# A two-layer hybrid backbone on one core: the first norm's rests all on VectorE and its values in place, the filter's products behind the modulation's, the first S5 steps' scratch below the filter

## The chip, the core and the metric

The kernel runs on one core of one Trainium2 chip. The time is device time of one execution in microseconds (us). Three runs of the kernel before took 1841.52 us (median; 1838.38 to 1842.83). A further execution was profiled: 1841.73 us, of which the trace spans 1839.8 us, so that 1.93 us lie around the span.

## The reference, cut to what matters

Two layers work on 256 context tokens and 256 latent tokens of width 1024, in float32. A vector of modulation values (shift, scale and gate for each half of a layer) comes from a small product with `ada_w`. The projected columns go to three mixers: a Fourier mix, a hyena mix (long convolutions whose filter is computed from weights) and S5 (a linear scan with complex states).

```python
for l in range(DEPTH):                                  # 2
    mod = silu(c) @ ada_w[l] + ada_b[l]                 # 6 rows of 1024, one set for each token kind
    h = modulate(rmsnorm(x, norm_mix_g[l]), sh_m, sc_m) # h * (1 + scale) + shift
    p = h @ w_in[l]                                     # to Fourier | hyena (3 x 384) | S5 (384)
    y = concat(fourier_mix(p_f), hyena_mix(p_h, k), s5(p_s)) @ w_out[l]
    x = x + g_m * y
    h = modulate(rmsnorm(x, norm_ffn_g[l]), sh_f, sc_f)
    x = x + g_f * (swiglu(h) if l == 0 else moe_top2_of_8(h))
return rmsnorm(x, final_g)

# hyena's filter: k = sine network of the position, times a decay, over its own sum of magnitudes
# S5: B_bar = ((exp(lam dt) - 1) / lam) * B, complex; h[t] = A_bar h[t-1] + B_bar u[t]; both directions
```

## The kernel before

**Numbers in two parts.** Layer 0's products are taken in three passes over rounded parts: a value x is held as xH (rounded) and xL = x - xH, its **rest**. The same holds for a weight (`wh`, `wl`; `wsplit`, L191 and L192). A product is hH.wh + hL.wh + hH.wl, so one column tile of the input projection is 24 matmuls of 512 columns (8 slices of the width, 3 passes). In the trace they are `pacc<-hH,wh`, `pacc<-hL,wh` and `pacc<-hH,wl`.

**The stages, by the trace.** 0 to about 62 us: the modulation's first rows (`ada_pe`, chunks 0, 2, 1, 3), the first half of hyena's filter (`hy_filter`), the first norm (`norm_h`) and S5's parameters (`s5_params`), whose tables of rotations `rotA` and `rotB` are one long chain of small operations on GpSimd. From 62 to about 295: layer 0's mixers (`mixers`): the projection's tiles m = 11, 12, 13 (S5's columns), 10, 2 and so on, S5 in sixths (`s5_mats` builds a sixth's matrices, `s5_sixth` runs its scan), and the hyena convolutions. To about 380: the out projection and the second norm; to about 800: the feed-forward part; to about 990: layer 1's mixers; to the end: eight experts, streamed from memory.

**What sets the order.** A scheduler of the tile framework puts each engine's instructions into one list, from the program's order and a cost model, and a list is worked strictly in its order. A tile taken from a pool that lies over a closed pool waits until all of the closed pool's readers and writers are done.

**The first norm** (`norm_h`, L468 to L503) holds its eight slices in `xin`. L492 multiplies them by 1/rms (VectorE). Then, for each slice: L499 (ScalarE) and L500 (VectorE) write the modulated values of the two token kinds into a tile `nf`, of which there are two; L501 (ScalarE) rounds it into `hH`; L502 subtracts into `hL`, on GpSimd and VectorE by turns.

**The filter** (`hy_filter`, L708 to L780) has two halves (one for each order). In each: two tiles of `hfb` (L753, VectorE), their sum `hs` and difference `hd` (L762, L763, GpSimd), the sum of magnitudes by TensorE (`psk<-ones,ab`), its reciprocal `rc` (L765, VectorE), the reciprocal spread by TensorE (`prk`) and copied to `rk` (L770, ScalarE), four products `pk` with `hs` and `hd` (TensorE), `Kf = pk * rk` (L777, VectorE), for two of the four an addition (L779, GpSimd), and a DMA to memory (L780, on SyncE's queue, `kd<-Kf`). Its pool `filt` is closed at the first S5 work, and the mixers' tiles `x2`, `U` and the ring `ar` of the modulation's later chunks lie over it.

**S5's sixth** (`s5_mats`): `bs`, `cs`, `d` are loaded (L566 to L568); L585 to L587 form `bre` and `bim` of 512 columns with a second product `x2` on GpSimd in layer 0 (L586; the trace calls the tile `x`); the scratch of these lies in a pool `scr` over S5's parameters' pool.
Of the kernel before, what the change touches and what calls it, by code (L numbers as in the profile page):

```python
# [8 lines left out]
F32 = mybir.dt.float32  # L9
# [7 lines left out]
D = 1024  # L17
# [118 lines left out]
def build(tc, A, out, dbg=None, upto='all'):  # L136
# [254 lines left out]
    def ada_pe(c, pool, cnt=[0]):  # L391
        pa = pt_('acc', (128, 512), "pad")
        for kh in range(2):
            cnt[0] += 1
            if cnt[0] % 2 or pool is None:
                r = load(A['adaN'][c][:, 4 * kh:4 * kh + 4], 4, 512)
            else:
                r = pool.tile([128, 4, 512], F32, name="raw2", tag="raw2", bufs=2)
                SP.dma_start(r, A['adaN'][c][:, 4 * kh:4 * kh + 4])
            for k in range(4):  # L400
                mm(pa[32 * k:32 * k + 32], scol32[:, 8 * kh + 2 * k:8 * kh + 2 * k + 32], r[:, k], kh == 0, kh == 1)
        row = (pool or wraw).tile([128, 512], F32, name="adr", tag="adr" if pool else "raw", bufs=1 if pool else 2)
        act(row, pa, AF.Copy)
        pt = pa[:, 0:8].rearrange("p (j s) -> p j s", s=2)
        for j in range(4):
            mm(pt[:, j], row[:, 128 * j:128 * j + 128], sum4, j == 0, j == 3, skip_group_check=True)
        act(mods[0][:, 4 * c:4 * c + 4], pt, AF.Copy)
        mods_done(0, 4 * c, 4)

# [19 lines left out]
    def ada(l, m0, m1, eng, pool):  # L429
        for m in range(m0, m1):  # L430
            r = pool.tile([128, D], F32, name="ar", tag="ar", bufs=2)
            SP.dma_start(r, A['adaT'][l, m])
            for s in range(1 if l == 1 and m >= 16 else 0, 2):
                o = mods[l][:, m, s:s + 1]
                if eng(m, s) == 'v':
                    jk = par.tile([128, D], mybir.dt.bfloat16, name="jk", tag="jk", bufs=1)
                    stt(jk, r, 1.0, crow[:, s], op0=mul, op1=mul, accum_out=o)
                else:
                    pd = par.tile([128, D], F32, name="pd", tag="pd", bufs=1)
# [28 lines left out]
    def norm_h(l, w, x, hH, hL, pool, inplace=False, **kw):  # L468
# [27 lines left out]
        for k in range(KD):  # L496
            u = us[k] if inplace else unit(k)
            f = tmp.tile([128, 512], F32, name="nf", tag="t512b", bufs=2)
            act(f[:, 0:256], u[:, 0:256], AF.Identity, bias=mods[l][:, sh0 + k, 0:1], scale=Gm[l][w][:, k, 0:1])  # L499
            ts_(f[:, 256:512], u[:, 256:512], Gm[l][w][:, k, 1:2], mods[l][:, sh0 + k, 1:2], op0=mul, op1=add)  # L500
            act(hH[:, k], f, AF.Copy)  # L501
            (gtt, tt_)[k % 2](hL[:, k], f, hH[:, k].bitcast(F32), op=sub)  # L502
# [55 lines left out]
    def s5_mats(p, l, q, M, rh, rd):  # L558
# [25 lines left out]
        for i, (src, op) in enumerate(((bre, sub), (bim, add))):  # L584
            tt_(src, bt(PB[0]), bh(bb[:, i]), op=mul)  # L585
            (tt_ if l else gtt)(x2, bt(PB[1]), bh(bb[:, 1 - i]), op=mul)  # L586
            tt_(src, src, x2, op=op)  # L587
            pt = pt_('mat', (128, 4, 128), "pbt")
            for g in range(4):
                PE.transpose(pt[:, g], src[:, g].rearrange("p t h -> p (t h)"), ident)  # L590
            act(M[:, :, 128 * i:128 * i + 128], pt, AF.Copy)
# [116 lines left out]
    def hy_filter(p, l, kd):  # L708
# [33 lines left out]
        for o_ in range(2):  # L742
# [40 lines left out]
    def mixers(l, hH, hL, z2, yH, yL, fill):  # L783
# [84 lines left out]
        def conv(p, K, src0, src1):  # L868
# [115 lines left out]
        with tc.tile_pool(name=f"s5p{l}", bufs=1, side="right") as p, banks(mat=2, s5=2):  # L984
# [36 lines left out]
            ysT = z2.tile([128, 3, n], F32, name="ysT", tag="ysT")  # L1021
# [16 lines left out]
            ms = [mats(0), mats(1)]  # L1038
# [5 lines left out]
            for th in range(3):  # L1044
                Y = p.tile([128, 4 if l == 0 else 2, 128], F32, name="Y")
                for h in range(2):
# [3 lines left out]
                    if l == 0 and q == 4:  # L1050
                        SC.close()
# [42 lines left out]
    z_es = ExitStack()  # L1094
    with tc.tile_pool(name="filt", bufs=1) as p_:
# [7 lines left out]
        with tc.tile_pool(name="prm", bufs=1) as p2_, tc.tile_pool(name="start", bufs=1) as st, banks(f=3, fk=1):  # L1103
# [9 lines left out]
            filt = hy_filter(p_, 0, kdr[0])  # L1113
# [13 lines left out]
    with z_es:  # L1127
# [3 lines left out]
        with tc.tile_pool(name="z0p", bufs=1) as z2, tc.tile_pool(name="ada0", bufs=1) as p_:  # L1131
# [9 lines left out]
            mixers(0, hH, hL, z2, yH, yL, fill0)  # L1141
# [689 lines left out]
```

## Time and profile before

| | |
|---|---|
| median of three runs | 1841.52 us |
| profiled execution | 1841.73 us, span 1839.8 us |
| TensorE busy (PE; PEld is its weight load) | 1714.5 us, 93% |
| VectorE (DVE) | 805.9 us, 44% |
| ScalarE (ACT) | 429.4 us, 23% |
| GpSimd (POOL) | 518.4 us, 28% |
| granted TensorE clock, mean over the span | 0.965 |

SyncE (SP) issues DMAs. The shares are means over stages with different limits. The granted clock is 1.0 at 2.4 GHz and 0.5 at 1.2 GHz. A row of a timeline holds the start, the duration, the engine, the line, the operation, out<-in, and in square brackets how long the engine was idle before it and for whom it waited. Nearly all matmuls have line L148, that of a helper, so they are told apart by their tiles.

### The profile page before, as it was taken

The page shows a single profiled execution, that of the slowest core. Times are in us where ns is not written, and L with a number is a line of the kernel's source. Part 1 is how long each engine was busy: PE and PEld are TensorE (multiplying, and loading weights), DVE is VectorE, ACT ScalarE, POOL GpSimd, SP SyncE. Part 2 cuts the span into 40 slices and gives each one's busy share as a digit, 9 for nine tenths or more (in the row PEclk, how much of TensorE's full clock was granted, in tenths as well). Part 3 has the DMA queues.
Part 4 walks back from the last instruction along what each step waited for, and adds up shares of the span by engine and source line. Part 5 has one row for each costly group of instructions (what it writes and reads, how often), then busy time and mean ns, then how long its engine had stood idle before and what let it go on. Part 6 is the DMA issues. An engine that isn't in the chain of part 4 may idle for free. (4 is left out here: it accounts for less than half of the span.)

```text
span 1839.8 us, 47195 instructions
## 1 busy us (share of the span) xinstructions
PE 1714.5 (93%) x20825; PEld 1193.8 (65%) x20825; DVE 805.9 (44%) x1502; ACT 429.4 (23%) x776; POOL 518.4 (28%) x512
## 2 busy tenths in 40 slices
PE   7988899899998998999998999999999989999984
PEld 4665667867766776788777656666666656666642
DVE  7589968875776667363853001111111101011102
ACT  4332324455444443232231000000000000000001
POOL 5965535567877676000420000000000000000000
PEclk7998999999999999999998999999999999999998
DMA  8244345434557555354649999999999999999994
GB/s 297 87 116 126 94 148 177 144 106 145 168 180 248 190 194 194 120 162 141 191 150 419 405 394 418 419 420 419 419 419 418 419 419 419 418 413 413 412 419 160
DMA packets 145461, 506.80 MB, mean 275 GB/s; under 512 B 18590, under 2 KB 71648, under 8 KB 101216
## 3 DMA queue, kind: packets, MB, share of 16 engines
q1 hardware_dynamic: 145248, 503.70, 72.0%
q8 instruction: 165, 2.70, 0.6%
q14 instruction: 48, 0.39, 0.1%
HBM read 489.34 MB, written 14.32 MB: 274 GB/s over the span
## 5 line engine op out<-in xcount | busy, mean ns | idle before, releaser
L148 PE MATMUL pgu<-raw,xe 128*32 128x256 f32 x9408 | 528.2, 379 | 12.2 <-DMA raw<-in_mwp_dram 11.4
L148 PEld LDWEIGHTS pgu<-raw,xe 128*32 128x32 f32 x9408 | 316.3, 110 | 209.5 <-DMA raw<-in_mwp_dram 15.1
L1652 DVE TENSOR_TENSOR sg<-sg,pgu 128x384 f32<-128x384 f32 (+1 forms) x56 | 28.2, 504 | 629.8 <-ACT sg L1651 629.8
L148 PE MATMUL py<-raw,hT 128*32 128x256 f32 x4704 | 270.0, 379 | 8.3 <-DMA raw<-in_mwp_dram 8.2
L440 POOL TENSOR_TENSOR pd<-ar,crow 128x1024 f32<-128x1024 f32 x88 | 226.6, 2575 | 105.4 <-ACT pd L441 83.9
L1547 POOL TENSOR_TENSOR ob<-ob,fgb 128x512 f32<-128x512 f32 x1 | 1.3, 1262 | 880.4 <-ACT ob L1546 880.4
L148 PEld LDWEIGHTS py<-raw,hT 128*32 128x32 f32 x4704 | 156.0, 110 | 110.4 <-DMA raw<-in_mwp_dram 7.9
L192 DVE TENSOR_TENSOR wl<-raw,wh 128x1024 fp32r<-128x1024 f32 x95 | 169.2, 1783 | 72.4 <-ACT wh L191 70.5
L1651 ACT ACTIVATE sg<-pgu 128x384 f32<-128x384 f32 (+1 forms) x56 | 25.2, 450 | 705.6 <-PE pgu L148 705.6
L148 PE MATMUL pgu<-fhL,wh 128*128 128x512 f32 (+1 forms) x376 | 146.2, 389 | 5.1 <-DVE fhL L538 5.1
L148 PE MATMUL pgu<-fhH,wh 128*128 128x512 f32 (+1 forms) x392 | 147.6, 387 | 1.4 <-ACT sg L1283 0.8
L148 PE MATMUL pgu<-fhH,wl 128*128 128x512 f32 (+1 forms) x360 | 142.1, 396 | 3.3 <-DVE wl L192 3.3
L191 ACT ACTIVATE wh<-raw 128x1024 fp32r<-128x1024 f32 x95 | 99.9, 1054 | 147.1 <-PE pacc L148 67.3
L441 ACT ACTIVATE pd<-pd 128x1024 f32<-128x1024 f32 x88 | 93.0, 1057 | 123.9 <-POOL pd L440 121.1
L148 PE MATMUL pacc<-HH,wh 128*128 128x512 f32 (+1 forms) x192 | 76.8, 401 | 14.2 <-DVE xT L1227 10.0
L148 PEld LDWEIGHTS pgu<-fhL,wh 128*128 128x128 f32 x376 | 72.2, 192 | 22.9 <-DVE fhL L538 6.4
L148 PEld LDWEIGHTS pgu<-fhH,wh 128*128 128x128 f32 x392 | 74.0, 193 | 16.6 <-issue 1.1
L148 PEld LDWEIGHTS pgu<-fhH,wl 128*128 128x128 f32 x360 | 68.1, 189 | 23.0 <-issue 4.7
L148 PE MATMUL pacc<-HL,wh 128*128 128x512 f32 (+1 forms) x192 | 74.6, 389 | 0.0
L148 PE MATMUL pacc<-HH,wl 128*128 128x512 f32 (+1 forms) x192 | 73.7, 390 | 0.3 <-DVE wl L192 0.3
L148 PE MATMUL pacc<-h,wm 128*128 128x256 f32 x272 | 64.5, 391 | 1.2 <-ACT h L549 1.2
L148 PEld LDWEIGHTS pacc<-h,wm 128*128 128x128 f32 x272 | 51.5, 194 | 9.0 <-ACT h L549 1.4
(583 smaller groups left out, 2410.8 us busy)
## 6 DMA issues: line engine op xcount, KB each, us to landing
raw<-in_mwp_dram SPq DMA_DIRECT2D x336, 1024.0 KB
ar<-in_adaT_dram SPq DMA_DIRECT2D x64, 512.0 KB
raw<-in_fwg_dram SPq DMA_DIRECT2D x11, 1024.0 KB
raw<-in_fwu_dram SPq DMA_DIRECT2D x11, 1024.0 KB
raw<-in_fwd_dram SPq DMA_DIRECT2D x11, 1024.0 KB
raw<-in_adaN_dram SPq DMA_DIRECT2D x8, 1024.0 KB
ar<-in_adaN_dram SPq DMA_DIRECT2D x16, 512.0 KB
raw<-in_w_out_dram SPq DMA_DIRECT2D x8, 1024.0 KB
```

Of the source, the lines that this page charges most:

```text
L148: return PE.matmul(o, l, r, start=start, stop=stop, **kw)
L191: act(h, r, AF.Copy)
L192: tt_(l, r, h.bitcast(F32), op=sub)
L440: gtt(pd, r, crow[:, s], op=mul)
L441: act(pd, pd, AF.Copy, accum_out=o)
L1547: gtt(o_, o_, fgb[:, hs], op=mul)
L1651: act(sg[:, 0:n], p[:, 0:n, 0:128], AF.Silu)
L1652: tt_(sg[:, 0:n], sg[:, 0:n], p[:, 0:n, 128:256], op=mul)
```

## The change

The parts below are made at once.

- `norm_h`: the modulated values are written into `xin` itself (no `nf`), and all eight rests are on VectorE. Its last rest is handed out as `done`.
- `s5_mats`: the two products `x2` of the first sixth are on VectorE.
- `hy_filter`: layer 0's products `pk` of both halves may be issued only behind the last matmul of `ada_pe(3)` (`sum4`; the trace writes `pad<-sum,adr`). Its sine network's scratch shares places with `ab`, `hd`, `hs`.
- A new pool `u0` below the filter's pool holds `U`, `ysT`, the scratch of `s5_mats` and the first hyena tiles' temporaries (four tiles with one buffer each that share places with `bre`, `x2`, `bim`, `y2`). The pool `scr` is gone. The matrices of the first two sixths are issued behind `done`.
- `ada`'s scratch (`jk`, `pd`) moves into the pool that its caller hands in.

```diff
@@ ada_pe
-            mm(pt[:, j], row[:, 128 * j:128 * j + 128], sum4, j == 0, j == 3, skip_group_check=True)
+            last = mm(pt[:, j], row[:, 128 * j:128 * j + 128], sum4, j == 0, j == 3, skip_group_check=True)
...
+        return last
@@ ada
-                    jk = par.tile([128, D], mybir.dt.bfloat16, name="jk", tag="jk", bufs=1)
+                    jk = pool.tile([128, D], mybir.dt.bfloat16, name="jk", tag="jk", bufs=1)
...
@@ norm_h
-            f = tmp.tile([128, 512], F32, name="nf", tag="t512b", bufs=2)
-            act(f[:, 0:256], u[:, 0:256], AF.Identity, bias=mods[l][:, sh0 + k, 0:1], scale=Gm[l][w][:, k, 0:1])
-            ts_(f[:, 256:512], u[:, 256:512], Gm[l][w][:, k, 1:2], mods[l][:, sh0 + k, 1:2], op0=mul, op1=add)
-            act(hH[:, k], f, AF.Copy)
-            (gtt, tt_)[k % 2](hL[:, k], f, hH[:, k].bitcast(F32), op=sub)
+            act(u[:, 0:256], u[:, 0:256], AF.Identity, bias=mods[l][:, sh0 + k, 0:1], scale=Gm[l][w][:, k, 0:1])
+            ts_(u[:, 256:512], u[:, 256:512], Gm[l][w][:, k, 1:2], mods[l][:, sh0 + k, 1:2], op0=mul, op1=add)
+            act(hH[:, k], u, AF.Copy)
+            rest = tt_(hL[:, k], u, hH[:, k].bitcast(F32), op=sub)
+        done.append(rest)
@@ s5_mats
-            (tt_ if l else gtt)(x2, bt(PB[1]), bh(bb[:, 1 - i]), op=mul)
+            (tt_ if l or q == 0 else gtt)(x2, bt(PB[1]), bh(bb[:, 1 - i]), op=mul)
@@ hy_filter
-            a = p.tile([64, 256], F32, name=nm + "a", tag="sina")
+            a = p.tile([64, 256], F32, name=nm + "a", tag="ab")
...
-                for t in range(2):
-                    mm(pk, fck[:, t, f // 2, (f % 2) * 128:(f % 2) * 128 + 128],
-                       (hs if f < 2 else hd)[:, t], t == 0, t == 1)
+                with tc.issue_after(after[0].ins) if after else nullcontext():
+                    for t in range(2):
+                        mm(pk, fck[:, t, f // 2, (f % 2) * 128:(f % 2) * 128 + 128],
+                           (hs if f < 2 else hd)[:, t], t == 0, t == 1)
@@ mixers
-            SC = ExitStack()
-            if l == 0:
-                scr = SC.enter_context(tc.tile_pool(name="scr", bufs=1, side="right"))
-            U = z2.tile([128, S5G, 4, 16], F32, name="U", tag="ysT")
+            U = (scr or z2).tile([128, S5G, 4, 16], F32, name="U", tag="ysT")
...
-            ms = [mats(0), mats(1)]
+            with tc.issue_after(behind.ins) if behind else nullcontext():
+                ms = [mats(0), mats(1)]
@@ the start
+    u0 = u_es.enter_context(tc.tile_pool(name="u0", bufs=1))
     with tc.tile_pool(name="filt", bufs=1) as p_:
...
+            after.append(ada_pe(3, st))
...
-            mixers(0, hH, hL, z2, yH, yL, fill0)
+            mixers(0, hH, hL, z2, yH, yL, fill0, u0, done[0])
+        u_es.close()
```

The engines' lists differ up to the middle of layer 0's feed-forward part and are the same behind it. Three places follow.

TensorE, around the first rest; `pad<-sum_88,adr` is `sum4` of `ada_pe(3)`. Before, then now:

```order
L148 MATMUL pk<-hs,ck 128x384 x3
L148 MATMUL pk<-hd,ck 128x384 x2
L148 MATMUL pad<-sum_88,adr 128x2 x4
L148 MATMUL pacc<-hH,wh 128x512
L148 MATMUL prk<-ident,rc 128x128 x3
L148 MATMUL pacc<-hL,wh 128x512
```
```order
L148 MATMUL pad<-sum_88,adr 128x2 x4
L148 MATMUL pk<-hs,ck 128x384 x4
L148 MATMUL pk<-hd,ck 128x384 x2
L148 MATMUL pacc<-hH,wh 128x512 x2
L148 MATMUL prk<-ident,rc 128x128 x3
L148 MATMUL pacc<-hL,wh 128x512
```

The modulation's last sum now stands ahead of all of the filter's products, one of which stood earlier before.

GpSimd, end of the rotation chain (`rtu`, `rtv`, `rotA`) and the filter's second half (the memset of `hfb`, then `hs` and `hd` twice). Before, then now:

```order
L755 MEMSET hfb 1x384
...
L762 TENSOR_TENSOR hs<-hfb 128x384
L763 TENSOR_TENSOR hd<-hfb 128x384
...
L762 TENSOR_TENSOR hs<-hfb 128x384
L248 TENSOR_TENSOR rotA<-rtu,rtv 128x48x2
L763 TENSOR_TENSOR hd<-hfb 128x384
...
L247 TENSOR_TENSOR rtv<-rotA,gen 128x192
L623 TENSOR_TENSOR M<-rotA,rotB 128x4x64 x4
L248 TENSOR_TENSOR rotA<-rtu,rtv 128x48x4
```
```order
L247 TENSOR_TENSOR rtv<-rotA,gen 128x192
L756 MEMSET hfb 1x384
L624 TENSOR_TENSOR M<-rotA,rotB 128x4x64 x2
L248 TENSOR_TENSOR rotA<-rtu,rtv 128x48x4
L763 TENSOR_TENSOR hs<-hfb 128x384
L764 TENSOR_TENSOR hd<-hfb 128x384
L596 TENSOR_TENSOR M<-cs,PC_108 128x4x128
L599 TENSOR_TENSOR M<-bb,PC_109 128x4x128
...
L763 TENSOR_TENSOR hs<-hfb 128x384
L764 TENSOR_TENSOR hd<-hfb 128x384
```

The filter's second half stood inside the chain and now stands behind all of it, and its second pair behind part of the first sixth's matrices.

VectorE, from the filter's second reciprocal to its first `Kf` (before), and from the last rests to the same place (now). `u`, `bb`, `bre`, `bim`, `x` and `M` belong to the first sixth:

```order
L765 RECIPROCAL rc<-psk 128x3
...
L585 TENSOR_TENSOR bre<-PB_106,bb 128x512
L248 TENSOR_TENSOR bb<-u_1115,u_1116 128x64
L585 TENSOR_TENSOR bim<-PB_106,bb 128x512
L192 TENSOR_TENSOR wl<-raw,wh 128x1024
L597 TENSOR_TENSOR M<-M,y_1125 128x4x128
...
L777 TENSOR_TENSOR Kf<-pk,rk 128x384 x2
```
```order
L502 TENSOR_TENSOR hL<-xin,hH 128x512 x2
L243 TENSOR_TENSOR u_1107<-bs,wre 128x64
...
L586 TENSOR_TENSOR bre<-PB_106,bb 128x512
L248 TENSOR_TENSOR bb<-u_1107,u_1108 128x64
L587 TENSOR_TENSOR x_1116<-PB_107,bb 128x512
L586 TENSOR_TENSOR bim<-PB_106,bb 128x512
...
L766 RECIPROCAL rc<-psk 128x3
L601 TENSOR_TENSOR M<-M,y_1117 128x4x128
L192 TENSOR_TENSOR wl<-raw,wh 128x1024
L779 TENSOR_TENSOR Kf<-pk,rk 128x384 x4
```

The first sixth's work stood between the second reciprocal and the second half's `Kf`, and now nearly all of it stands ahead of the reciprocal.

## Rows read from the trace of the kernel before

**Rows 1.** The page, part 1: busy time, share of the span, instructions.
```profile
PE 1714.5 (93%) x20825; PEld 1193.8 (65%) x20825; DVE 805.9 (44%) x1502; ACT 429.4 (23%) x776; POOL 518.4 (28%) x512
```

**Rows 2.** Stretches: length, busy time (instructions) of each engine, granted clock, DMA share, GB/s.
```profile
57.00:124.00 67.00, 59.27 (x405) 42.56 (x406) 38.40 (x66) 24.19 (x43) 56.73 (x91) 0.92 0.34 105
...
120.00:230.00 110.00, 95.50 (x938) 65.61 (x934) 102.52 (x216) 33.79 (x65) 60.94 (x71) 0.92 0.37 109
...
990.00:1839.00 849.00, 809.91 (x14866) 501.37 (x14856) 116.52 (x250) 44.16 (x101) 1.26 (x1) 0.99 0.98 402
```

**Rows 3.** Timeline of TensorE: start, duration, operation, idle before.
```profile
56.81 0.95 PE L148 MATMUL pad<-sum,adr 128*128 128x2 f32 x8
...
61.97 0.79 PE L148 MATMUL pacc<-hL,wh 128*128 128x512 f32 x1 [3.20 <-POOL hL L502]
...
79.98 1.39 PE L148 MATMUL psk<-ones,ab 128*128 128x1 f32 x12
...
87.53 1.39 PE L148 MATMUL psk<-ones,ab 128*128 128x1 f32 x12
...
93.53 0.83 PE L148 MATMUL prk<-ident,rc 128*128 128x128 f32 x6
```

**Rows 4.** Two shorter stretches, columns as in rows 2.
```profile
62.00:65.40 3.40, 3.40 (x8) 2.72 (x9) 2.43 (x7) 2.89 (x7) 3.40 (x10) 0.50 0.02 5
65.40:80.00 14.60, 14.60 (x53) 9.01 (x53) 7.60 (x18) 6.53 (x12) 14.59 (x30) 1.00 0.15 54
```

**Rows 5.** GpSimd by line, 57 to 124 us: busy, mean ns, idle before.
```profile
L502 POOL TENSOR_TENSOR hL<-nf,hH 128x512 fp32r<-128x512 f32 x4 | 5.7, 1435 | 0.0
```

**Rows 6.** Timeline of GpSimd.
```profile
74.94 0.41 POOL L755 MEMSET hfb<- 1x384 f32 x1
...
75.95 0.99 POOL L762 TENSOR_TENSOR hs<-hfb 128x384 f32<-128x384 f32 x1
76.91 1.00 POOL L763 TENSOR_TENSOR hd<-hfb 128x384 f32<-128x384 f32 x1
...
79.26 1.00 POOL L762 TENSOR_TENSOR hs<-hfb 128x384 f32<-128x384 f32 x1
...
80.63 1.98 POOL L763 TENSOR_TENSOR hd<-hfb 128x384 f32<-128x384 f32 x1
...
87.56 0.53 POOL L247 TENSOR_TENSOR rtv<-rotA,gen 128x192 f32<-128x192 f32 x1
```

**Rows 7.** VectorE by line, 57 to 124 us.
```profile
L192 DVE TENSOR_TENSOR wl<-raw,wh 128x1024 fp32r<-128x1024 f32 x5 | 8.9, 1771 | 1.2 <-ACT wh L191 1.2
...
L502 DVE TENSOR_TENSOR hL<-nf,hH 128x512 fp32r<-128x512 f32 x4 | 3.0, 748 | 1.7 <-ACT hH L501 1.7
```

**Rows 8.** Timeline of VectorE.
```profile
56.27 0.76 DVE L502 TENSOR_TENSOR hL<-nf,hH 128x512 fp32r<-128x512 f32 x1
...
61.95 0.74 DVE L500 TENSOR_SCALAR nf<-xin,G,mods 128x256 f32<-128x256 f32 x2 [4.92 <-POOL hL L502]
...
73.05 0.69 DVE L502 TENSOR_TENSOR hL<-nf,hH 128x512 fp32r<-128x512 f32 x1
...
94.09 1.55 DVE L585 TENSOR_TENSOR bre<-PB,bb 128x512 f32<-128x512 f32 x1
...
96.68 0.70 DVE L585 TENSOR_TENSOR bim<-PB,bb 128x512 f32<-128x512 f32 x1
...
101.03 1.01 DVE L777 TENSOR_TENSOR Kf<-pk,rk 128x384 f32<-128x384 f32 x2
...
107.58 0.55 DVE L777 TENSOR_TENSOR Kf<-pk,rk 128x384 f32<-128x384 f32 x1
...
109.37 0.47 DVE L841 SCALAR_TENSOR_TENSOR hq<-pacc,colp,hq 128x255 f32<-128x255 f32 x1
...
125.70 0.41 DVE L655 TENSOR_TENSOR w<-pv,M 128x256 f32<-128x256 f32 x1
```

**Rows 9.** Timeline of ScalarE.
```profile
112.74 1.08 ACT L1012 ACTIVATE U<-pU 128x512 f32<-128x512 f32 x2 [3.15 <-DMA kd<-Kf]
```

More of the change, by code (lines that the diff above doesn't have):

```diff
@@ L1 @@
 import math
-from contextlib import ExitStack, contextmanager
+from contextlib import ExitStack, contextmanager, nullcontext
 import concourse.bass as bass
@@ L435, in ada @@
                 if eng(m, s) == 'v':
-                    jk = par.tile([128, D], mybir.dt.bfloat16, name="jk", tag="jk", bufs=1)
+                    jk = pool.tile([128, D], mybir.dt.bfloat16, name="jk", tag="jk", bufs=1)
                     stt(jk, r, 1.0, crow[:, s], op0=mul, op1=mul, accum_out=o)
                 else:
-                    pd = par.tile([128, D], F32, name="pd", tag="pd", bufs=1)
+                    pd = pool.tile([128, D], F32, name="pd", tag="pd", bufs=1)
                     gtt(pd, r, crow[:, s], op=mul)
@@ L465, in rsqrt_small, with norm_h @@
         return y
-    def norm_h(l, w, x, hH, hL, pool, inplace=False, **kw):
+    def norm_h(l, w, x, hH, hL, pool, inplace=False, done=None, **kw):
         pst = pt_('aux', (128, 4), "pst")
@@ L705, in s5_out, with hy_filter @@
             pt.rearrange("p t (q c) -> p t q c", q=nq), AF.Copy, scale=0.5)
-    def hy_filter(p, l, kd):
+    def hy_filter(p, l, kd, after=()):
         fzT, fdec, fck = const(p, 'czT'), const(p, 'cdec'), const(p, 'ck')
@@ L721, in sine @@
         def sine(src, b, fr, nm):
-            a = p.tile([64, 256], F32, name=nm + "a", tag="sina")
-            i = p.tile([64, 256], I32, name=nm + "i", tag="sini")
-            nf = p.tile([64, 256], F32, name=nm + "n", tag="sinn")
+            a = p.tile([64, 256], F32, name=nm + "a", tag="ab")
+            i = p.tile([64, 256], I32, name=nm + "i", tag="hd")
+            nf = p.tile([64, 256], F32, name=nm + "n", tag="hs")
             o_ = p.tile([64, 256], F32, name=nm + "o", tag="sino", bufs=2)
@@ L780, in hy_filter, with mixers @@
                 SP.dma_start(kd[:, o_, f], K)
-    def mixers(l, hH, hL, z2, yH, yL, fill):
+    def mixers(l, hH, hL, z2, yH, yL, fill, scr=None, behind=None):
         t0 = 0 if l == 0 else 256
@@ L876, in conv @@
             for f in range(2):
-                ta, tb, tc_, td = (p.tile([128, HY], F32, name=n_, tag=n_, bufs=b_) for n_, b_ in
-                                   (("t_a", 2), ("t_b", 1), ("t_a", 2), ("t_b", 1)))
+                ta, tb, tc_, td = ((scr or p).tile([128, HY], F32, name=n_, tag=g_ if scr else n_, bufs=1 if scr else b_)
+                                   for n_, g_, b_ in (("t_a", "bre", 2), ("t_b", "x2", 1), ("t_a", "bim", 2), ("t_b", "y2", 1)))
                 tt_(ta, pu[f], K[:, f], op=mul)
@@ L1020, in mixers @@
                 act(X[:, 8 * q:8 * q + 8], px, AF.Copy)
-            ysT = z2.tile([128, 3, n], F32, name="ysT", tag="ysT")
+            ysT = (scr or z2).tile([128, 3, n], F32, name="ysT", tag="ysT")
             order = HYO[l]
@@ L1050, in mixers @@
                     if l == 0 and q == 4:
-                        SC.close()
                         mes[0].close()
@@ L1093, in build @@
     rdr = [dr.tile([32, 4, 240], F32, name=f"rd1{q}") for q in range(6)]
-    z_es = ExitStack()
+    z_es, u_es = ExitStack(), ExitStack()
+    u0 = u_es.enter_context(tc.tile_pool(name="u0", bufs=1))
     with tc.tile_pool(name="filt", bufs=1) as p_:
@@ L1112, in build @@
                     act(crow[:, s, 512 * h:512 * h + 512], pb.rearrange("p a b -> p (a b)"), AF.Copy)
-            filt = hy_filter(p_, 0, kdr[0])
+            after = []
+            filt = hy_filter(p_, 0, kdr[0], after)
             next(filt)
@@ L1118, in build @@
                 SP.dma_start(xin[:, 2 * q:2 * q + 2], A['xT'][:, 2 * q:2 * q + 2])
-            nrm = norm_h(0, 0, xin, hH, hL, st, True)
+            done = []
+            nrm = norm_h(0, 0, xin, hH, hL, st, True, done)
             next(nrm)
             ada_pe(1, st)
-            ada_pe(3, st)
+            after.append(ada_pe(3, st))
             next(nrm)
```

## The prediction, made before the changed kernel was run

> **What bounds the kernel now.** I read the shares on the page first, then the busy time by stretches, then the waits and the timelines from 50 to 130 us, where the change works. The page says that TensorE is busy for 93% of the span [rows 1], but that is an average over stages. From 990 us to the end, the experts, the DMA share is 0.98 at 402 GB/s [rows 2]: the change touches nothing there, and the lists are the same from the middle of the feed-forward part on. So a gain can only come from before, as a lead with which all that follows starts earlier. From 120 to 230 us, S5's scans, VectorE is busy for 102.5 of 110 us, TensorE for 95.5 [rows 2]: VectorE is the bound there, and what counts is how early it enters. From 57 to 124 us nothing is full: VectorE is busy for 38.4 of 67 us [rows 2], 28.6 us idle, so waits set the time. Two stand out.
>
> The first is at 61.97: TensorE stands 3.2 us for the first rest, which GpSimd makes [rows 3]. The same instruction holds VectorE for 4.92 us before 61.95, since there are only two `nf` tiles [rows 8]. Right behind that pause the granted clock is 0.50, which is 1.2 GHz, for 3.4 us, and 1.00 from then to 80 us [rows 4].
>
> The second is at 112.74: ScalarE's copy into `U` stood 3.15 us for the DMA of the filter's last `Kf`, since `U` lies where the filter's tiles were [rows 9]. That DMA was issued after the last `Kf` at 107.58 [rows 8]. The first scan product on VectorE comes at 125.70, 13.0 us behind `U` [rows 8, 9].
>
> **The change part by part.** The sum is made on the profiled execution, 1841.73 us with 1.93 us around its span; it lies 0.2 us above the median of the runs.
>
> *Modulation ahead of the filter's products.* `sum4` ran at 56.81, behind ten matmul records of the filter's products [rows 3]. Now it stands first, so the last modulation values come earlier by what these take, and the products, unchanged in number, follow. They cost nothing new: TensorE idles 3.2 us behind them today [rows 3].
>
> *Rests in place, all on VectorE.* GpSimd loses four rests, 5.7 us at 1435 ns [rows 5]. VectorE gains four at 748 ns [rows 7], 3.0 us. The first rest no longer waits for GpSimd's chain. VectorE began its own first rest at 56.27 [rows 8]; now two more modulated values (0.74 us for the two at 61.95 [rows 8]) and two operations on the modulation's values stand before it, so it ends at an estimated 58.6. TensorE stood from 61.97 - 3.2 = 58.8 on [rows 3]; now one product and one `hH` pass more lie before that point, about 1.2 us, so it reaches the rest at 60.0 and finds it made: 2.0 us before 61.97. With the pause gone I take the clock to stay at 1.00: the 3.4 us slow stretch held 8 matmuls [rows 4], which at half the time are 1.7 us, 1.7 saved (bounds 0 and 3.4, as the fall could come elsewhere). With the second `hH` pass drawn ahead and the small gaps of that stretch, TensorE ends the projection's first two tiles, 79.98 before [rows 3], about 5 us earlier (2 to 6.5).
>
> *Products `x2` of the first sixth.* VectorE takes two more operations of the kind that took 0.70 us alone and 1.55 us beside GpSimd [rows 8]: 1.4 to 3.1 us. With the rests VectorE has 4.4 us more work (up to 9.3 if rests too took 1.55), against 28.6 idle us. I take 4.4, as the four rests of before took 748 ns while GpSimd was busy for 56.7 of 67 us [rows 2, 7]. Should that idle time be gone, the 4.4 us are on the path.
>
> *The filter's second half behind the rotation chain.* This speaks against the change at first. `hd` of the second pair ended at 82.61 before [rows 6]. Now: the chain's last table step, ended at 88.09 [rows 6], comes earlier by the four rests (5.7) [rows 5], the two pairs of `hs` and `hd` (0.99, 1.00, 1.00, 1.98) and a memset (0.41) [rows 6] that no longer stand before it: 88.1 - 11.1 = 77.0. Behind it come the memset, three operations and the first pair, to 81.2, then some 6 us of the first sixth's matrices and the second pair: `hd` ends at 89.1, 6.5 us later than before. But what followed shrinks. Before, 4.9 us passed until TensorE reached `psk` at 87.53, then 6.0 us to `prk` at 93.53, and `Kf` began at 101.03 [rows 3, 8], 7 us after the spread reciprocal, because `bre`, `bim`, `wl` and `M` stood ahead of it on VectorE. Now that work is done before the second half's reciprocal. Counted by TensorE's list, `psk` comes before the second pair's products; nine passes (0.2 us each, half of what 8 took in 3.4 us [rows 4]) and `prk` follow those, and `rk` is there at about 93; `Kf` begins at 94, 7 us earlier than at 101.03. If the 6.5 us from there to the last `Kf` and its DMA stay, the filter's release comes at about 105.7 instead of 112.7: 7 us earlier (bounds: 7 later, if nothing shrinks, and 10 earlier). For this release wait `x2` on ScalarE and the ring `ar` on SyncE's queue, and behind `ar` on that queue the first sixth's `rd` and `M`.
>
> *Scratch and `U` below the filter.* `U` does not wait for the release any more; it follows `prk` at about 94 to 97. With the 13.0 us from `U` to the first scan product [rows 8, 9] that product is at 107 to 113 (more passes now lie between), say 110, where it was 125.70 [rows 8]. This is not all gain, as work that stood ahead of it now stands behind it: one `wl` (1.77 us [rows 7]), three operations of 512 columns (0.70 to 1.55 each [rows 8]) and four of the convolution's (0.47 each [rows 8]), 5.8 to 8.3 us. VectorE enters its full stretch with a lead of 15.7 - 7.1 = 8.6 us (4 to 13).
>
> *Four single buffers for the convolution's temporaries, and `ada`'s scratch in another pool.* Each is one buffer as before or two made one; the products with two buffers lie in the stretch where VectorE is the bound, which works its list in order, so I put 0 (bounds 0.5 gained by memory coming free, and 2 lost).
>
> *Sum.* Three leads: TensorE 5, the release 7, VectorE 8.6. The release and VectorE gate the stretch from 120 us; TensorE has slack in it. I take the smaller of the two, 7.0 us: 1841.7 - 7.0 = 1834.7 us.
>
> On the port there is a rule that speaks against the rests on VectorE. The trace has the same operation at 1.55 and 0.70 us [rows 8]. The Trainium skill, page "SBUF — State Buffer", section "Who interferes with whom", states that a VectorE instruction with two SBUF inputs and a GpSimd instruction that reads SBUF contend for one pair of ports, and that the one issued second is blocked until the first has finished. The trace agrees for the pair above, but the rests of before, at 748 ns beside a GpSimd that hardly paused, show little of it. By the rule each rest would pay for what is left of one GpSimd operation; the rival below is made from rows.
>
> **The rivals.**
>
> *Given back.* The rests run at 1.55 instead of 0.75 us, eight of them: 6.4 us more. The last rest was begun at 73.05 [rows 8]; freed of `nf` and GpSimd it would come at about 69, and with 6.4 us more at about 75. Then the first sixth's work behind it, `wl` and `Kf` slide by 6, and the lead is 0.5 to 2 us: 1840.5 us. For it: 1.55 at 94.09. Against it: 748 ns in the mean.
>
> *Slower: the late second pair.* TensorE's list has the products with the second `hs` ahead of a whole column tile's remaining passes and of S5's first small products. If the 25.5 us from 82.61 to the end of the last `Kf` (108.13) [rows 6, 8] do not shrink, because TensorE stands before those products and VectorE behind them, then 89.1 + 25.5 = 114.6: the release is 6.5 us later than before, and `x2`, `ar` and the two accumulators held by them with it: 1848.2 us. It decides as soon as the last `Kf` ends after 108.1. For it: the order shown, and GpSimd's fullness (56.7 of 67 us [rows 2]). Against it: 12 of the 25.5 us (4.9 before `psk`, 7 before `Kf`) were waits for work that now stands ahead.
>
> *More.* The clock stays up beyond the first projections and all of VectorE's 13 us count: 12 us, 1829.7 us.
>
> **How the numbers follow.** Forecast (gain of 5.5 to 10) 0.56, given back 0.26, late pair 0.14, more 0.04. A measurement of this kernel can tell 0.3%, 5.5 us, from no change: faster 0.60, same 0.26, slower 0.14. The range reaches to 1826 at the low side, which leaves out part of "more", and to 1845 at the high side, which takes in all of "given back" and leaves out most of the late pair; the likeliest case alone is 1831 to 1836.
>
> **What would show it.** Right: TensorE's first `pacc<-hL,wh` at about 60 without a wait for GpSimd and a granted clock near 1.00 from 62; rests near 750 ns; the first tiles ended near 75; `Kf` of the second half from about 94 and `ar` issued near 106; the first scan product near 110; from 230 us on every event some 7 us earlier. Wrong: rests over 1.2 us; a wait of TensorE for `hs` near 88; a last `Kf` after 108; or a lead at 125 that is gone at 230, which would mean that something other than VectorE's entry bounds the stretch.

## The result: slower by 1.0%, and the profile after

The changed kernel takes 1858.23 us (median of 4 runs, 1856.96 to 1862.46), the kernel before 1842.08 in the runs beside it: a ratio of 1.0099 (95% interval 1.0082 to 1.0115). The forecast was 1834.7, in a range of 1826 to 1845. The profiled execution spans 1857.4 us against 1839.8, 17.6 more.

Its busy time (page, part 1) and the stretches that answer to [rows 2, 4] are these:

```profile
PE 1728.0 (93%) x20825; PEld 1203.4 (65%) x20825; DVE 815.5 (44%) x1508; ACT 428.6 (23%) x776; POOL 519.4 (28%) x506
```
```profile
57.00:124.00 67.00, 62.33 (x408) 45.20 (x407) 43.90 (x72) 23.75 (x43) 46.50 (x81) 0.91 0.28 92
120.00:230.00 110.00, 90.63 (x833) 62.46 (x831) 99.30 (x205) 32.50 (x61) 65.72 (x73) 0.84 0.38 114
...
62.00:65.40 3.40, 3.40 (x17) 2.47 (x16) 0.18 (x2) 0.15 (x1) 3.32 (x14) 1.00 0.02 5
52.00:62.00 10.00, 10.00 (x31) 6.74 (x32) 10.00 (x19) 5.94 (x12) 9.59 (x23) 0.52 0.00 1
```

VectorE is busy for 43.9 us from 57 to 124 us, not 38.4, and for 99.3 of 110 us from 120 to 230, not 102.5: it is busier in front of its full stretch and idles more within it. The granted clock is 1.00 from 62 to 65.4 us, as forecast, but 0.52 in the ten us before; from 120 to 230 us it is 0.84, where it was 0.92 before.

TensorE's timeline, for [rows 3]:

```profile
56.67 1.85 PE L148 MATMUL pad<-sum,adr 128*128 128x2 f32 x8
...
64.97 0.48 PE L148 MATMUL pacc<-hL,wh 128*128 128x512 f32 x1
...
85.07 2.38 PE L148 MATMUL psk<-ones,ab 128*128 128x1 f32 x12 [2.75 <-ACT ab L758]
...
103.25 0.83 PE L148 MATMUL prk<-ident,rc 128*128 128x128 f32 x6
```

`sum4` is first now, at 56.67, but no earlier than before: the granted clock is 0.50 from 27.4 us on, up to 61.6. The first rest is used at 64.97 without a wait, 3 us later than before instead of 2 earlier. At 85.07 TensorE stands 2.75 us for `ab`, which waits for a memset on GpSimd. `prk` comes at 103.25, before at 93.53.

The rests (VectorE by line, 57 to 124 us), for [rows 7], and VectorE's timeline, for [rows 8]:

```profile
L502 DVE TENSOR_TENSOR hL<-xin,hH 128x512 fp32r<-128x512 f32 x8 | 5.7, 763 | 0.0
```
```profile
85.99 7.85 DVE L192 TENSOR_TENSOR wl<-raw,wh 128x1024 fp32r<-128x1024 f32 x1 [3.75 <-ACT wh L191]
...
104.65 1.02 DVE L779 TENSOR_TENSOR Kf<-pk,rk 128x384 f32<-128x384 f32 x2 [3.63 <-ACT rk L771]
...
110.01 0.56 DVE L779 TENSOR_TENSOR Kf<-pk,rk 128x384 f32<-128x384 f32 x1 [1.19 <-PE pk L148]
...
119.86 0.42 DVE L656 TENSOR_TENSOR w<-pv,M 128x256 f32<-128x256 f32 x1
...
246.49 0.42 DVE L656 TENSOR_TENSOR w<-pv,M 128x256 f32<-128x256 f32 x1 [0.18 <-PE pv L148]
...
271.44 0.56 DVE L907 TENSOR_TENSOR za<-ia,pi 128x384 f32<-128x384 f32 x1 [3.89 <-ACT ia L905]
```

A rest takes 763 ns in the mean, so the rests are not blocked. But one `wl`, at 85.99, takes 7.85 us. The second half's `Kf` begins at 104.65, 3.6 us later than before, and the last starts at 110.01. The first scan product, `w<-pv,M`, is 5.8 us earlier (119.86), the last, 246.49, is 13 us later; `za`, the hyena's first product behind the stage's last transforms, is at 271.44, 10.8 us later than before (260.60).

GpSimd's timeline from the end of the rotation chain on, for [rows 6]:

```profile
83.73 0.41 POOL L756 MEMSET hfb<- 1x384 f32 x1
...
85.83 0.99 POOL L763 TENSOR_TENSOR hs<-hfb 128x384 f32<-128x384 f32 x1
86.78 0.99 POOL L764 TENSOR_TENSOR hd<-hfb 128x384 f32<-128x384 f32 x1
87.74 1.05 POOL L596 TENSOR_TENSOR M<-cs,PC 128x512 f32<-128x512 f32 x1
...
92.71 0.10 POOL L627 MEMSET rh<- 128x4 f32 x1
...
94.86 1.38 POOL L763 TENSOR_TENSOR hs<-hfb 128x384 f32<-128x384 f32 x1 [2.06 <-DVE hfb L754]
96.19 1.00 POOL L764 TENSOR_TENSOR hd<-hfb 128x384 f32<-128x384 f32 x1
```

The memset and the first pair stand behind the chain, as the list said. From 85.83 to 92.81 GpSimd runs eleven instructions without a pause, and the `wl` of 85.99 ends 1 us behind them. The tiles `hfb` stand behind that `wl` on VectorE, so `hs` waits 2.06 us for them, and the second `hd` ends at 97.19, forecast 89.1, before 82.61.

ScalarE's last copy into `U`, and the ring's first DMA behind the filter's release on SyncE's queue, for [rows 9]:

```profile
104.60 0.60 ACT L1012 ACTIVATE U<-pU 128x512 f32<-128x512 f32 x1
```
```profile
112.60 0.83 SPq L416 DMA_DIRECT2D ar<-in_adaN_dram  x2
```

`U` has no wait any more, but the release (112.60) is where it was (112.71).

Where the 17.6 us arise, by the starts of the same events, of which the scan products are each the first of a sixth: first sixth -5.8 us, third (169.05 against 159.96) +9.1, last +13.0, out projection's first pass (307.99 against 292.84) +15.2, feed-forward's first (366.97 against 353.27) +13.7, first expert's (1004.8 against 988.1) +16.7. So most of the loss is made between 120 and 310 us.

### The profile page after: what moved, and what is told of

Its sections match the earlier page's. It is cut to its first block, busy times and chain, and to the rows that moved or that the text cites. A ratio compares the mean times of both kernels' runs of the same rounds, so it can differ in the third digit from the quotient of the medians.

```text
span 1857.4 us, 47182 instructions
## 1 busy us (share of the span) xinstructions
PE 1728.0 (93%) x20825; PEld 1203.4 (65%) x20825; DVE 815.5 (44%) x1508; ACT 428.6 (23%) x776; POOL 519.4 (28%) x506
## 5 line engine op out<-in xcount | busy, mean ns | idle before, releaser
L148 PE MATMUL pgu<-raw,xe 128*32 128x256 f32 x9408 | 530.4, 379 | 12.6 <-DMA raw<-in_mwp_dram 12.1
L191 ACT ACTIVATE wh<-raw 128x1024 fp32r<-128x1024 f32 x95 | 99.8, 1054 | 144.0 <-PE pacc L148 72.5
```

The costliest lines, as they stand in the source:

```text
L148: return PE.matmul(o, l, r, start=start, stop=stop, **kw)
L191: act(h, r, AF.Copy)
```

## The experiments

Sixteen kernels in four groups. "List share" is how many of VectorE's instructions stand in the same sequence as in the kernel before (longest match, of some 2145); the changed kernel has 91.3%. The starts are those of the first rest on TensorE, of the first scan product of the first, third and last sixth on VectorE, and of the out projection on TensorE. They are read from one execution of each kernel, and the early ones vary from one execution to the next: up to 120 us the lists of e11 and e12 are those of before, and the first rest is used at 61.97, 65.22 (e11, TensorE's row) and 60.37 (e12).

```profile
65.22 0.48 PE L148 MATMUL pacc<-hL,wh 128*128 128x512 f32 x1
```

| | time us | ratio to before (95%) | list share | first rest | scan products 1, 3, last | out proj. |
|---|---|---|---|---|---|---|
| before | 1842 | | | 61.97 | 125.70, 159.96, 233.54 | 292.8 |
| changed | 1858.2 | 1.0099 (1.0082-1.0115) | 91.3% | 64.97 | 119.86, 169.05, 246.49 | 308.0 |
| e1 norm only | 1851.4 | 1.0063 (1.0043-1.0082) | 89.5% | 59.56 | 122.02, 166.58, 236.62 | 301.6 |
| e2 no u0 | 1848.3 | 1.0039 (1.0024-1.0054) | 88.6% | 62.86 | 127.15, 166.02, 240.66 | 297.6 |
| e3 free products | 1852.6 | 1.0063 (1.0045-1.0081) | 85.2% | 59.86 | 111.38, 165.50, 238.86 | 297.1 |
| e4 sixth behind filter | 1864.1 | 1.0126 (1.0108-1.0144) | 88.5% | 60.83 | 115.44, 170.42, 247.81 | 314.4 |
| e5 products only | 1839.8 | 0.9989 (0.9975-1.0002) | 99.8% | 59.93 | 125.87, 159.96, 232.52 | 292.8 |
| e6 x2 only | 1860.0 | 1.0100 (1.0075-1.0124) | 94.3% | 62.40 | 124.93, 163.03, 240.95 | 307.5 |
| e7 memory only | 1858.1 | 1.0079 (1.0050-1.0108) | 86.0% | 65.33 | 118.55, 161.66, 241.38 | 300.7 |
| e8 first rest | 1842.2 | 1.0008 (0.9994-1.0021) | 98.0% | 57.10 | 127.36, 163.52, 233.19 | 295.0 |
| e9 third rest | 1853.0 | 1.0058 (1.0040-1.0077) | 89.9% | 62.32 | 126.06, 169.72, 235.62 | 301.1 |
| e10 products, two rests | 1841.4 | 0.9997 (0.9987-1.0007) | 97.5% | 59.53 | 124.32, 160.38, 231.13 | 295.1 |
| e11 order only, q = 2 | 1851.7 | 1.0053 (1.0037-1.0070) | 95.1% | 65.22 | 127.43, 162.90, 246.53 | 301.6 |
| e12 order only, q = 3 | 1851.4 | 1.0059 (1.0040-1.0078) | 95.7% | 60.37 | 123.79, 157.74, 226.11 | 298.0 |

### Parts undone: e1 to e4

The first question was whether the 80 to 115 us (late second half, blocked `wl`: theory L) or the new memory (theory M) made the loss.

e1, on the kernel before:
```diff
-            f = tmp.tile([128, 512], F32, name="nf", tag="t512b", bufs=2)
...
+            tt_(hL[:, k], u, hH[:, k].bitcast(F32), op=sub)
```


> The kernel before with the norm's part alone: values in place, all eight rests on VectorE; products, x2 and memory as before. Theory L (the loss is made between 80 and 115 us: GpSimd's second filter half comes late and a wl of VectorE is blocked beside a GpSimd that does not pause, 7.85 us in the changed kernel): the first rest is not waited for any more, the filter's second half moves late in GpSimd's list here too, so between 2 us faster and 4 us slower than before, 1840 to 1846. Theory M (the loss comes from the new memory u0, whose tiles bind S5's scratch and the convolution's temporaries together): this part alone gains what the prediction said, 1836 to 1840.

1851.4 us: 10 slower, outside both. The first rest comes 2.4 us earlier and the first scan product 3.7, and still the out projection begins 8.8 later.

e2, on the changed kernel (old pools and the temporaries' own buffers again):
```diff
-    u0 = u_es.enter_context(tc.tile_pool(name="u0", bufs=1))
+            if l == 0:
+                scr = SC.enter_context(tc.tile_pool(name="scr", bufs=1, side="right"))
```


> The changed kernel with the old memory: scratch of the sixths in its own pool over S5's parameters, U and ysT in the mixers' pool, the convolution's temporaries with their own buffers. Rests, x2, the products behind sum4 and the order behind the last rest stay as changed. Theory M: the loss behind 150 us goes, 1840 to 1847. Theory L: it stays, 1853 to 1860.

1848.3: 10 us of the loss go, 6 stay, between the two theories.

e3, on the changed kernel:
```diff
-            filt = hy_filter(p_, 0, kdr[0], after)
+            filt = hy_filter(p_, 0, kdr[0])
```


> The changed kernel without the order of the filter's products behind sum4. GpSimd's memset of hfb stands before the chain's last steps here and the first pair hs, hd comes earlier. Theory L: TensorE's 2.75 us stand for ab and the slow clock behind it go, and the wl is blocked for less: 1850 to 1855. Theory M: no change, 1855 to 1860.

1852.6, within L's range: 5.6 us of the loss go, 11 stay. No `wl` is blocked here (the longest between 83 and 108 us takes 1.64 us). VectorE's timeline has the first scan product 14.3 us earlier than before, that of the third sixth 5.5 later and that of the last 5.3 later:

```profile
111.38 0.42 DVE L656 TENSOR_TENSOR w<-pv,M 128x256 f32<-128x256 f32 x1
...
165.50 0.41 DVE L656 TENSOR_TENSOR w<-pv,M 128x256 f32<-128x256 f32 x1
...
238.86 0.42 DVE L656 TENSOR_TENSOR w<-pv,M 128x256 f32<-128x256 f32 x1 [0.36 <-PE pv L148]
```

A lead of 14 us, near the 15.7 that the forecast has for this event, is used up by the third sixth. TensorE's longest wait from 120 to 180 us (total, times, longest) is for the DMA that brings S5's `M` back from memory; that of before stands below it:

```profile
PE py L148 <- DMA M<-rd: 9.4, 2, 5.3
...
PE py L148 <- DMA M<-rd: 0.5, 2, 0.3
```

So at this entry S5's steps wait for more than VectorE.

e4, on the changed kernel:
```diff
+                with tc.issue_after(HD[0][-1].ins) if behind else nullcontext():
-                ms = [mats(0), mats(1)]
+                    ms = [mats(0), mats(1)]
```


> The changed kernel with GpSimd's instructions of the first two sixths issued behind the filter's last hd, so that GpSimd pauses between the filter's two pairs. Theory L: the wl takes about 1.7 us instead of 7.85, hs and hd of the second pair end near 89, the last Kf comes 6 to 8 us earlier: 1848 to 1853. Theory M: the entry moves but the total stays within 3 us, 1855 to 1859.

The edit did what it was made for. GpSimd's timeline (first two rows) has a pause of 1.14 us between the pairs, and the same `wl` on VectorE takes 1.22 us:

```profile
85.48 0.99 POOL L766 TENSOR_TENSOR hd<-hfb 128x384 f32<-128x384 f32 x1
87.61 1.91 POOL L765 TENSOR_TENSOR hs<-hfb 128x384 f32<-128x384 f32 x1 [1.14 <-DMA raw<-in_w_in_dram]
```
```profile
87.45 1.22 DVE L192 TENSOR_TENSOR wl<-raw,wh 128x1024 fp32r<-128x1024 f32 x1
```

The time rose to 1864.1, outside both ranges: with the block gone and the second `hd` ended at 90.5, the kernel is 6 us slower than the changed one. So the blocked `wl` does not make the loss. The last `Kf` starts at 109.04, only 1.0 us earlier than in the changed kernel, where 6 to 8 were expected, so the late second half is not tested here; in e3, where the last `Kf` starts 6.5 us earlier, 11 of the 16 us stay. M is not shown either. What e1 to e4 share is that the scheduler wrote the mixers' lists anew for each: theory O.

### Parts alone: e5 to e8

e5, on the kernel before, has the `issue_after` of the products as the change has it.

> The kernel before with the filter's products behind sum4 alone. VectorE's list stays the same but for 0.2% of its rows. Theory O (the loss is made by the lists: every part makes the scheduler write the mixers' lists anew, and any new lists fit the chip worse than those of before by 5 to 15 us): since the lists stay, no loss, 1838 to 1843. Theory P (the parts themselves cost: products later, filter late): 1844 to 1848.

1839.8, no measurable difference. TensorE (first row) uses the first rest 2.0 us earlier, without a wait (a difference that lies within what e11 and e12 show for equal lists); VectorE's last `Kf` and first scan product are where they were [rows 8]:

```profile
59.93 0.50 PE L148 MATMUL pacc<-hL,wh 128*128 128x512 f32 x1
```
```profile
107.15 0.55 DVE L779 TENSOR_TENSOR Kf<-pk,rk 128x384 f32<-128x384 f32 x1
...
125.87 0.41 DVE L656 TENSOR_TENSOR w<-pv,M 128x256 f32<-128x256 f32 x1
```

So the lead of 2 us at 60 us does not reach 125 us even where the lists stay: the second pair's `hd` on GpSimd ended at 81.33, before at 82.61, and the last `Kf` is 0.4 us earlier.

e6, on the kernel before:
```diff
-            (tt_ if l else gtt)(x2, bt(PB[1]), bh(bb[:, 1 - i]), op=mul)
+            (tt_ if l or q == 0 else gtt)(x2, bt(PB[1]), bh(bb[:, 1 - i]), op=mul)
```


> The kernel before with the first sixth's two products x2 on VectorE alone. Direct cost: 2 operations of 0.70 to 1.55 us on VectorE, 2 of 2.04 us less on GpSimd, so between 2 us faster and 3 us slower (theory P: 1839 to 1844). VectorE's list differs in 6% of its rows all through the mixers; theory O: 1845 to 1852.

1860.0: two instructions moved, both done by 107 us, cost 18 us, as much as the whole change. VectorE's scan products, and TensorE's longest waits from 180 to 305 us (total, times, longest):

```profile
124.93 0.41 DVE L655 TENSOR_TENSOR w<-pv,M 128x256 f32<-128x256 f32 x1
...
163.03 0.41 DVE L655 TENSOR_TENSOR w<-pv,M 128x256 f32<-128x256 f32 x1
...
240.95 0.42 DVE L655 TENSOR_TENSOR w<-pv,M 128x256 f32<-128x256 f32 x1
```
```profile
PE pbt L590 <- DVE bim L587: 6.0, 2, 3.8
PE pacc L148 <- DVE x L842: 3.1, 1, 3.1
PE py L148 <- DMA M<-rd: 2.5, 1, 2.5
```

At 125 us it is 0.8 us ahead, at the third product 3.1 behind, at the last 7.4, at the out projection 14.7: the loss grows where nothing was moved between engines. TensorE stands 6.0 us in front of `pbt`, for `bim`, and 3.1 for the hyena's `x`, where before no wait of that stretch is longer than 1.5 us: transposes and passes stand in its list ahead of what VectorE's list brings late. The time is above theory O's range (1845 to 1852), which had the loss too small.

e7, on the kernel before: `u0`, the shared places and `ada`'s scratch as in the change.

> The kernel before with the new memory alone: u0 below the filter, the convolution's temporaries sharing places with the sixths' scratch, sine scratch on shared places, ada's scratch in its caller's pool. Theory O: VectorE's list differs in 14% of its rows, 1847 to 1857. Theory M (shared places bind S5 and the convolution): 1848 to 1858 as well, with VectorE or GpSimd waiting for a convolution's product before bre or bim. Theory P without M: U is free of the filter's release, 1836 to 1842.

1858.1, at the upper end of M's range (0.1 us above it) and 1 us above O's, with a first scan product 7.2 us earlier. P without M is out. M's sign, VectorE or GpSimd waiting for a convolution's product before `bre` or `bim`, is not in the trace, but between O and M the time decides nothing.

e8, on the kernel before:
```diff
-            (gtt, tt_)[k % 2](hL[:, k], f, hH[:, k].bitcast(F32), op=sub)
+            (tt_ if k == 0 else (gtt, tt_)[k % 2])(hL[:, k], f, hH[:, k].bitcast(F32), op=sub)
```


> The kernel before with only the first rest moved from GpSimd to VectorE; nf as before. TensorE's 3.2 us wait for the first rest and the slow clock behind it go. VectorE's list differs in 2% of its rows. Theory O: lists nearly kept, so the lead stays: 1837 to 1841. Theory W (VectorE and TensorE wait for each other all through the sixths, so that any lead at 80 us is used up by 160 us): 1840 to 1843.

1842.2, the same as before: 1 us above theory O's range and within theory W's. The first rest is 4.9 us earlier, the first scan product 1.7 later, so the lead does not stay, as O had it; no cost comes with it either.

### One rest, two rests, and order alone: e9 to e12

e9 is e8 with `k == 2` in place of `k == 0`.

> The kernel before with one rest alone moved to VectorE, that of the third slice (k = 2); nf as before. Direct cost: one operation of 0.75 us more on VectorE at about 64 us and 1.75 us less on GpSimd, so within 1 us of before if the operation itself decides (theory P: 1840 to 1844). VectorE's list differs in 10% of its rows up to 290 us, as those of the slower kernels do. Theory O: 1847 to 1858.

e10 is e5 with the rests of `k in (0, 2)` on VectorE.

> The kernel before with the products behind sum4 and two rests on VectorE (k = 0 and k = 2). More is moved than in the kernel with the third rest alone, but VectorE's list differs in 2.5% of its rows. Theory O: not slower than before, 1837 to 1843. Theory P: the third rest costs the same here as alone, whatever that is.

1853.0 and 1841.4. The one moved rest whose lists changed (89.9% the same) costs 11 us; two moved rests, that one among them, whose lists nearly stay (97.5%) cost nothing. Theory P, as the expectations name it, falls.

e11 and e12, on the kernel before, with `q in (2,)` and `q in (3,)`; `S6` holds the last VectorE instruction of a sixth's scan:
```diff
-                        hy_tile(order[done], raws)
+                        with tc.issue_after(S6[-1].ins) if l == 0 and q in (2,) else nullcontext():
+                            hy_tile(order[done], raws)
```


> The kernel before with no instruction added, removed or moved to another engine: VectorE's part of the hyena tile at the third sixth (q = 2) may only be issued behind the sixth's scan. VectorE's list differs in 5% of its rows from about 134 us on; all before that is the same. Theory O: 1846 to 1858, with first scan product, filter and first rest as before. Theory P: no part of the change is here, 1839 to 1844.

> As the last one, but at the fourth sixth (q = 3): VectorE's list differs in 4% of its rows from about 166 us on. Theory O: 1844 to 1856. Theory P: 1839 to 1844.

1851.7 and 1851.4, both 10 us slower, with the same instructions on the same engines. (The edge binds VectorE's instructions alone, but the other engines' lists come out new from there on too.) In e11 the first rest and the first scan product are not as before but 3.3 and 1.7 us later, though VectorE's list is still the same there. e12 shows how a part of the loss comes. VectorE's timeline there:

```profile
123.79 0.41 DVE L657 TENSOR_TENSOR w<-pv,M 128x256 f32<-128x256 f32 x1
...
150.62 1.64 DVE L192 TENSOR_TENSOR wl<-raw,wh 128x1024 fp32r<-128x1024 f32 x1
...
201.80 2.36 DVE L192 TENSOR_TENSOR wl<-raw,wh 128x1024 fp32r<-128x1024 f32 x2
...
226.11 0.42 DVE L657 TENSOR_TENSOR w<-pv,M 128x256 f32<-128x256 f32 x1
...
240.23 0.47 DVE L845 SCALAR_TENSOR_TENSOR x<-pacc,colp,x 128x252 f32<-128x252 f32 x1
...
263.73 1.22 DVE L192 TENSOR_TENSOR wl<-raw,wh 128x1024 fp32r<-128x1024 f32 x1 [6.51 <-ACT wh L191]
266.34 0.56 DVE L907 TENSOR_TENSOR za<-ia,pi 128x384 f32<-128x384 f32 x1 [1.31 <-ACT ia L905]
```

And that of the kernel before:

```profile
152.53 1.64 DVE L192 TENSOR_TENSOR wl<-raw,wh 128x1024 fp32r<-128x1024 f32 x1
...
176.47 1.23 DVE L192 TENSOR_TENSOR wl<-raw,wh 128x1024 fp32r<-128x1024 f32 x1
...
229.60 0.47 DVE L842 SCALAR_TENSOR_TENSOR x<-pacc,colp,x 128x252 f32<-128x252 f32 x1
...
233.54 0.42 DVE L655 TENSOR_TENSOR w<-pv,M 128x256 f32<-128x256 f32 x1
...
257.93 1.40 DVE L192 TENSOR_TENSOR wl<-raw,wh 128x1024 fp32r<-128x1024 f32 x1 [0.76 <-PE pyT L148]
...
260.60 0.56 DVE L904 TENSOR_TENSOR za<-ia,pi 128x384 f32<-128x384 f32 x1 [0.81 <-ACT ia L902]
```

In e12 the S5 steps are ahead, at last by 7.4 us (226.11 against 233.54). But the hyena's tiles are held: no `wl` comes between 150.62 and 201.80, where before there were three, at 176.47, 186.67 and 199.82, and the last of the convolution's operations on `hq` or `x` starts at 240.23 instead of 229.60. At 263.73 VectorE stands 6.51 us for ScalarE's `wh`, and `za` is 5.7 us later. The stage runs two streams, S5's sixths and the hyena's tiles, through the same VectorE and TensorE, and its end follows the later one here. Before, the starts of their last steps lie within 4 us of each other (233.54 and 229.60). Of e12's loss, 5.1 us stand at the out projection; the rest arises behind it (see what stays open).

### The changed kernel with other lists: e13 to e16

No work is changed, only one order edge: e13 holds `mats(1)` behind the filter's last `Kf`, e14, e15 and e16 are e11's edge at q = 1, 3 and 5.

> The changed kernel, no work changed, with VectorE's instructions of the second sixth's matrices only behind the filter's last Kf. VectorE's list differs from the changed kernel's in 10% of its rows, from 119 us on. Theory O: the time moves by more than 4 us from 1858, to either side (1845 to 1866). Theory P (the changed kernel's parts cost the 17 us, however the lists run): 1855 to 1861.

> The changed kernel, no work changed, with VectorE's part of the hyena tile of the second sixth only behind that sixth's scan. VectorE's list differs from the changed kernel's in 11% of its rows. Theory O: away from 1858 by more than 4 us to either side (1845 to 1866). Theory P: 1855 to 1861.

> As the last one, at the fourth sixth; the list differs from the changed kernel's in 7% of its rows, from about 180 us on, when the changed kernel is some 9 us late already. Theory O: 1848 to 1866, away from 1858. Theory P: 1855 to 1861.

> As the last one, at the last sixth; the list differs in 3% of its rows, from about 220 us on, and is nearer to that of the kernel before than the changed kernel's. Theory O: 1850 to 1862, if anything faster. Theory P: 1855 to 1861.

1855.0, 1866.3, 1872.6 and 1860.4 (ratios to before 1.0068, 1.0123, 1.0167 and 1.0092, intervals at most 0.0023 to either side). Two (e14 and e15) moved by more than the 4 us that theory O asked for, and end 0.3 and 6.6 us above its ranges; two (e13 and e16) stayed in theory P's range. So P, by which the lists do not matter, falls with e14 and e15, and O is not borne out in e13 and e16. With e3 and e4, which change only the order too, seven kernels of the same work (the changed one among them) take 1852.6 to 1872.6 us: the order is worth 20 us. None came below 1850, so the parts are not cleared.

## Why the prediction was wrong

**The step that failed** is the carrying of the lead: that VectorE "is the bound there, and what counts is how early it enters", so that the smaller lead at 120 us would be the gain. In place of a gain of 7 us the runs showed a lead of 5.8 us at the first scan product and a delay of 13.0 at the last sixth's. The prediction had named this sign of being wrong itself: a lead at 125 us that is gone at 230. In the kernel before, VectorE's stretch from 120 to 230 us is full with one particular sequence of its two streams in the lists, and the change wrote that sequence anew. The diff of the lists reached to the middle of the feed-forward part; the prediction read its first 125 us and gave the new sequence behind them no price, and its slower rival, the late second pair, covered only the entry (the last `Kf` did end after 108.1, at 110.57, but the release came no later). e3 (lead 14.3 us, 11 slower), e6 (lead 0.8, 18 slower) and e12 (S5 7.4 us ahead, 10 slower) show that the first scan product does not tell when the stage ends; e11 and e12 show that new lists alone, without any part of the change, cost 10 us, and e9 beside e10 that the same moved rest costs 11 us with new lists and nothing with nearly the old ones. That new lists make all of the changed kernel's loss is not shown.

**The first rest.** Forecast 60.0; 59.56 with the norm alone (e1), 59.93 with the products alone (e5), but 64.97 with all parts, where the clock was 0.52 from 52 to 62 us. Neither the hits nor the miss say much: with equal lists up to there e11 has 65.22, at a clock of 0.50 from 52 to 62 us, and e12 60.37, at 1.00. What came as forecast is that the wait for GpSimd is gone, the clock behind it (1.00 from 62 to 65.4 us) and the rests' 750 ns. The 5 us that TensorE was to gain on the projection's first two tiles did not come: their last pass starts at 80.97, before at 79.75. Such a lead was not on the path either: e5, e8 and e10 have 2.0 to 4.9 us at the first rest and no change in time.

**The filter's second half.** Forecast: `hd` 89.1, first `Kf` 94, release 105.7. Measured: 97.2, 104.65, 112.6. The order was as worked out, the times were not: the chain's last table step ended at 83.8, not 77.0, which is 6.8 of the 8.1 us by which `hd` is late. The sum left GpSimd's own operations at their old length, and some took longer (0.98 and 1.45 us for two steps, L244 and L245, that took 0.54 and 0.60). The rest comes with the `wl` that GpSimd blocked: it stands ahead of `hfb`, for which `hs` waits 2.06 us. With free products (e3) the last `Kf` starts at 103.50 and the ring's DMA at 106.07, near the forecast, and that alone did not bring a gain. The rival "given back" named the port, with the rests as its place; the place was a `wl`. The block did not decide the time: e4.

**U below the filter** did what was said at the entry: no wait, and the first scan product 5.8 us earlier, or 14.3 with free products (e3), where 15.7 was forecast.

**What stays open.** Kernels with new lists take 1848 to 1860 us without `u0` (e1, e2, e6, e9, e11, e12) and 1853 to 1873 with it (changed, e3, e4, e7, e13 to e16). Part of that may be the shared places. VectorE's waits of the changed kernel from 180 to 305 us have one, the last below, that none of the kernels without `u0` has:

```profile
DVE wl L192 <- ACT wh L191: 4.2, 3, 2.3
DVE za L907 <- ACT ia L905: 3.9, 1, 3.9
...
DVE t_b L886 <- DMA rd<-R: 1.7, 1, 1.7
```

A temporary of the convolution, `t_b`, waits for the DMA out of `R`, since both use the place of `y2`: 1.7 us here, 1.3 in e7, 3.3 in e3, 2.9 in e4, 5.4 in e16. In e13 to e15, which have `u0` too and take 1855.0 to 1872.6, it is absent, so it does not set the time. More than that was not shown. A kernel with `u0` and separate places was not run. Nor was the old sequence forced on the changed kernel, so how its 16 us divide between lists and memory is not settled.

Two more things are open. TensorE's granted clock from 120 to 300 us was 0.94 before, 0.91 in the changed kernel and 0.85 in e15, the slowest, so part of what an order costs may be paid as a slower clock; but e11 has 0.93 and is 10 us slower, and e5 has 0.92 and is not. And not all of the loss is made in the mixers. The feed-forward's first product is 4.9 us late in e12, 6.2 in e3, 8.9 in e9 and 9.7 in e7, the first expert's 7.6, 12.1, 14.8 and 16.9. Why the delay grows between them stays open.

## What to carry to other kernels

Where a scheduler writes the lists, compare the whole lists before and after, not only the place of the change: in a stage of two streams through the same engines, lists that were new in 4 to 15% of VectorE's rows cost 7 to 23 us here (e1 to e4, e6, e7, e9, e11, e12), and lists new in 2.5% or less cost nothing (e5, e8, e10). The share does not rank the losses: 18 us at 94.3% (e6), 11 at 85.2% (e3). A lead counts only at the event that ends the stage, so follow both streams to their last instruction. And try a part's neutral neighbour (e9 beside e10, e12 without any part) before its mechanism is blamed.

## What the runs showed of the hardware that was not expected

A VectorE product of 1024 columns with two inputs took 7.85 us while GpSimd ran eleven instructions without a pause, in the changed kernel, e14, e15 and e16 alike (7.85 or 7.86), 3.84 us in e13, where GpSimd's instructions stand in another order and it ended 1.1 us behind the third of them, and 1.22 us where GpSimd paused (e4). The Trainium skill, page "SBUF — State Buffer", section "Who interferes with whom", has the instruction that comes second blocked until the first finishes. The trace agrees that it is blocked, but here it stood through eleven instructions, not one; the measurement decides. Rests of 512 columns beside the rotation chain, whose operations depend on each other, took 763 ns in the mean; that the dependence is the reason was not shown.
